# Weights of each output tile at a start of their own, 12 to 120 bytes behind a multiple of 512

## The chip, the cores and the metric

One core of one Trainium2 chip. The metric is the device time of one execution in microseconds, as the median of several runs; the kernel before has 1240.85 us (3 runs, 1239.77 to 1241.22). Beside the runs stands one profiled execution, from which all durations below are taken.

## The reference

Two residual layers over a sequence of 512 tokens of width 1024, float32. Layer 0 mixes tokens with a grouped complex state-space layer (S5), layer 1 with causal forgetting attention (FoX, 16 heads of 64). Each is followed by a gated FFN with a causal convolution of width 3 over tokens. Every sub-layer is normed, scaled and shifted by a conditioning vector, and gated back into the stream.

```python
for i in range(DEPTH):                      # DEPTH = 2
    shift, scale, gate = adaln_params(c, ada_w[i, 0], ada_b[i, 0])
    hn = modulate(h, norm_g[i, 0], shift, scale)
    m = s5_mixer(hn, ...) if i % 2 == 0 else fox_mixer(hn, ...)
    h = h + gate * m
    shift, scale, gate = adaln_params(c, ada_w[i, 1], ada_b[i, 1])
    hn = modulate(h, norm_g[i, 1], shift, scale)
    h = h + gate * conv_ffn(hn, ...)
return rmsnorm(h, final_g)

def conv_ffn(h, w_up, conv_w, conv_b, w_down):
    a, b = jnp.split(h @ w_up, 2, axis=-1)  # D_FF = 2816 each
    ap = jnp.pad(a, ((0, 0), (CONV_W - 1, 0), (0, 0)))
    a_conv = conv_b
    for i in range(CONV_W):
        a_conv = a_conv + ap[:, i:i + S] * conv_w[i]
    return (jax.nn.silu(a_conv) * b) @ w_down
```

## The kernel before

Activations stand transposed in SBUF: 128 channels on the partitions, 512 tokens along each partition, `KT` = 8 such blocks for a width of 1024. A product with a weight matrix makes one output tile of 128 channels after the other. A tile's weights are `nk` blocks of 128 x 128 floats, which lie behind each other in one room, 512 bytes of each partition per block.

Matmuls run in the type fp32r. To keep float32's precision every operand is held as two parts: `put_parts` lets ScalarE copy it into a "hi" tile (L277), and VectorE subtracts that from the original into a "lo" tile (L278). Each block of a product is then three matmuls into the same PSUM tile (`mms`, L294): hi weights with hi activations, hi with lo, lo with hi. In all but one place the weights are the loaded side (LDWEIGHTS, PEld in the profile) and the activations the moving side.

The products by kind:

- **Plain products** (`product`, middle loop, L294): one tile of weights after the other, 512 moving columns. Up-projections of some FFN tiles, all down-projections but the last ones, the gate and output of S5, queries, keys and output of FoX.
- **Head and tail of `product`**: the first tiles of some products run together, block by block, in halves of 256 tokens in most cases, so that they can follow a norm that is finished by halves. The last two or four tiles also run in halves, so that the next norm can start early.
- **Quarters** (`quarters`, L550): most up-projections of the FFN, in pairs of tiles, are made by a scheme with seven products of half size instead of eight; each is 4 blocks of 3 matmuls with 256 moving columns, 84 matmuls a pair. 15 pairs of the first FFN and 18 of the second.
- **Values of FoX** (`fox_values`, L1361): here the activations are loaded and the weights move, 256 or 272 columns at a time.

Weights come by DMA into rooms named `raw` (issued by SyncE), are split into `w_hi` and `w_lo`, and these rotate through `WB` = 5 rooms each (in the tail: 4 rooms of another pool; one split of the quarters has a room in the FFN's pool). A room has `ROOM` = 9 x 128 floats, one block more than the eight of a full tile, so a tile may begin a little behind the room's start:

```python
    t = pool.tile([P, ROOM if bufs == WB else n * w + P], F32R, name=name, tag=tag, bufs=bufs)
    return t[:, aside:aside + n * w].rearrange("p (n w) -> p n w", w=w)
```

(`part_of`.) `aside` counts floats. Before, it is 0 for the plain products and the heads, and `ASIDE` = 16, which is 64 bytes, for tails, quarters and the values. The rooms themselves begin at multiples of 512 bytes.

The order of instructions on each engine is set by the tile framework's scheduler from the order in the code, with a few explicit `issue_after` edges. The rooms and who reads and writes them set the waits between the engines.

Of the kernel before, what the change touches and what calls it, by code (L numbers as in the profile page):

```python
# [9 lines left out]
F32R = mybir.dt.float32r  # L10
# [7 lines left out]
P = 128  # L18
# [19 lines left out]
RAW, WB = 3, 5  # L38
# [22 lines left out]
    pool.tile([P, n // 4], F32, name="fill", bufs=1)  # L61


ROOM, ASIDE = 9 * P, 16


def part_of(pool, shape, name, tag, bufs, aside=0):

    _, n, w = shape
    t = pool.tile([P, ROOM if bufs == WB else n * w + P], F32R, name=name, tag=tag, bufs=bufs)  # L70
    return t[:, aside:aside + n * w].rearrange("p (n w) -> p n w", w=w)


class Trunk:
# [223 lines left out]
    def product(self, w, ms, nk, x, evac, head=0, tail=0, after=None, ticks=0, halves=HALVES, tail_pool=(), first=None, step=None):  # L298


        ms = list(ms)
        full = slice(0, S)
        if head:
            wk = first or {m: self.weights(w[m], nk) for m in ms[:head]}
            ps = {m: self.mm.tile([P, S], F32, name="mmp") for m in ms[:head]}
            for c in halves:
                for k in range(nk):
                    for m in ms[:head]:
                        self.mms(ps[m][:, c], wk[m], x, k, nk, c)
                    self.finish_norm((k + 1) * head)  # L310
                    if step:
                        step(3)
            for m in ms[:head]:
                evac(m, ps[m], full)
                self.tick(ticks)
        for m in ms[head:len(ms) - tail]:
            wk = self.weights(w[m], nk)
            ps = self.mm.tile([P, S], F32, name="mmp")
            for k in range(nk):
                self.mms(ps, wk, x, k, nk, full)  # L320
                if step:
                    step()
            evac(m, ps, full)
            self.tick(ticks)
        if tail:
            last = ms[len(ms) - tail:]
            wk = {m: self.weights(w[m], nk, *tail_pool, aside=ASIDE) for m in last}
            for c in HALVES:
                for m in last:
                    if c is HALVES[1] and m == last[tail // 2]:  # L330
                        rb = self.rms_rows(y)
                    ps = self.mm.tile([P, S // 2], F32, name="mmp")
                    for k in range(nk):
                        self.mms(ps, wk[m], x, k, nk, c)
                    evac(m, ps, c)
                if c is HALVES[0]:
                    y = after[0](c)
                else:
                    y2 = after[0](c)
                    after[1](HALVES[0], y, rb)  # L340
            self.pending = lambda: after[1](HALVES[1], y2)
# [168 lines left out]
    def quarters(self, pool, l, f, x, finish):  # L510

        nc = self.nc
        H, N = KT // 2, S // 2
        t1, t2 = HALVES
        a, b = (self.raw([P, KT, P], self.io["w_up"][l][2 * f + j]) for j in range(2))
        a11, a12, a21, a22 = a[:, :H], a[:, H:], b[:, :H], b[:, H:]
        c, d = (pool.tile([P, 2, H, P], F32, name="sums", bufs=2) for _ in range(2))
        sub = lambda o, u, v, op=ALU.subtract: nc.vector.tensor_tensor(o, u, v, op)  # L518
        w = {}
        copied = self.copied  # L520

        def parts(src, names, *where):
            hi, lo = (
                pool.tile([P, H * P + P], F32R, name=n, tag="e" + n)[:, ASIDE:ASIDE + H * P].rearrange("p (n w) -> p n w", w=P)
                if where else part_of(self.wpool, [P, len(names) * H, P], n, n, WB, ASIDE)
                for n in ("w_hi", "w_lo")
            )
            with self.behind(*copied):
                self.put_parts(hi, lo, src)
            for j, n in enumerate(names):  # L530
                w[n] = hi[:, j * H:(j + 1) * H], lo[:, j * H:(j + 1) * H]

        parts(a, ("a11", "a12"))
        sub(c[:, 0], a21, a22, ALU.add)
        sub(c[:, 1], c[:, 0], a11)
        parts(c.rearrange("p n k m -> p (n k) m"), ("s1", "s2"))
        sub(d[:, 1], a11, a21)
        sub(d[:, 0], a12, c[:, 1])
        parts(d.rearrange("p n k m -> p (n k) m"), ("s4", "s3"))
        parts(a22, ("a22",), pool)  # L540
        quarter = lambda k, t: tuple(v[:, k * H:(k + 1) * H, t] for v in x)
        xs = {"b11": quarter(0, t1), "b21": quarter(1, t1), "b22": quarter(1, t2)}
        for n, v in self.tx.items():
            xs[f"t{n}"] = v

        def times(o, wn, xn, first=True):
            (whi, wlo), (xhi, xlo) = w[wn], xs[xn]
            for k in range(H):
                for n, (wt, xt) in enumerate(((whi, xhi), (whi, xlo), (wlo, xhi))):
                    self.last_mm = nc.tensor.matmul(  # L550
                        o, wt[:, k], xt[:, k], start=(first and k == 0 and n == 0), stop=(k == H - 1 and n == 2),
                        skip_group_check=True,
                    )

        def copy(o, last=False):
            t = self.tmp.tile([P, N], F32, name="nm_h", bufs=4)
            a = nc.scalar.activation(t, o, AF.Copy)  # L557
            if last:
                self.copied = [a.ins]
            return t  # L560

        p1, p5 = (self.mm.tile([P, S], F32, name="mmp")[:, :N] for _ in range(2))
        p2, p4 = (self.aux.tile([P, S], F32, name="aux")[:, :N] for _ in range(2))
        oa, ob = (self.tmp.tile([P, S], F32, name="nm_t") for _ in range(2))
        times(p1, "a11", "b11")
        c1 = copy(p1)
        times(p5, "s1", "t1")
        c5 = copy(p5)
        times(p2, "a12", "b21")
        sub(oa[:, t1], p2, c1, ALU.add)  # L570
        times(p1, "s2", "t2", False)
        c2 = copy(p1, True)
        times(p5, "s4", "b22", False)
        sub(oa[:, t2], p5, c2, ALU.add)
        finish(2 * f, oa, slice(0, S))
        times(p4, "a22", "t4")
        c4 = copy(p4)
        times(p1, "s3", "t3", False)
        sub(ob[:, t2], p1, c5, ALU.add)
        sub(ob[:, t1], p1, c4)  # L580
        finish(2 * f + 1, ob, slice(0, S))
# [98 lines left out]
class Ew:  # L680
# [29 lines left out]
    def sub(self, a, b, out=None):  # L710
        return self.tt(a, b, ALU.subtract, out)
# [577 lines left out]
class Kernel(S5):  # L1289
# [32 lines left out]
    def fox_values(self, pool, x):  # L1322
# [10 lines left out]
        def load(qs):  # L1333

            out = {q: [] for q in qs}
            for c in range(3):
                for q in qs:
                    src = self.io["fox_v"][q - 1] if q else self.io["fox_vf"]
                    n, step = (W, 4) if q else (W + NH, 3)
                    a = c * step  # L1340
                    j = min(step, KT - a)
                    if j <= 0:
                        continue
                    with self.behind(*(self.squared if 0 in qs and c else ())):
                        hi, lo = self.split(src[:, a:a + j, :], [P, j, n], aside=ASIDE)
                    out[q] += [(hi[:, i, :], lo[:, i, :]) for i in range(j)]
            return out

        def values(qs, blocks, w, aux=()):
# [15 lines left out]
            for q, b in todo:  # L1365
# [5 lines left out]
                if q == 0:  # L1371
                    nc.vector.tensor_tensor(ft[:, b, :], ps[q, b][:, W:W + NH], bf, ALU.add)

        w = load(range(2))
        self.tick(1)
        values((0, 1), (0, 1), w)
        values((0, 1), (2, 3), w, ((0, 2), (0, 3)))
        lf = self.log_forget(ft, pool)
        for q in range(2, NV):
            values((q,), range(NB), load([q]))  # L1380
# [260 lines left out]
```

## Time and profile before

| | |
|---|---|
| median of the runs | 1240.85 us |
| profiled execution, its own time | 1233.09 us |
| its span, first to last instruction | 1231.3 us |
| busy LDWEIGHTS (PEld) | 1031.2 us |
| busy ScalarE | 606.3 us |
| DMA moved | 183.83 MB, mean 149 GB/s |
| mean granted TensorE clock | 0.995 |

Costliest single groups of the page that belong to the products:

```profile
L294 PE MATMUL mmp<-ghi,w_hi 128*128 128x512 f32 (+1 forms) x392 | 145.1, 370 | 0.0
L550 PE MATMUL mmp<-w_hi 128*128 128x256 f32 x396 | 111.4, 281 | 2.6 <-ACT nm_h L557 2.6
L278 DVE TENSOR_TENSOR w_lo<-raw,w_hi 128x1024 fp32r<-128x1024 f32 (+4 forms) x173 | 183.3, 1065 | 35.4 <-ACT w_hi L277 34.8
```

A row of groups reads: line, engine, operation, output tile <- input tiles, shapes, count | busy us, mean ns of one | idle us of the engine just before them, and who ended it. The end of a matmul is modelled, and each starts before the one ahead is marked as ended; the pace of matmuls is therefore read from the distance of their starts, in the timeline. Stretches of the program by time: S5 to about 276 us, first FFN to 600, values of FoX to 690, attention to 860, second FFN to the end.

### The profile page before, as it was taken

What the parts mean: (1) busy time and instruction counts of PE and PEld (TensorE: products, weight loads), DVE (VectorE), ACT (ScalarE), POOL (GpSimd) and SP (SyncE); (2) the same over time, 40 slices, a digit from 0 to 9 for tenths busy, and PEclk for the clock granted to TensorE, in tenths of its full rate; (3) what the DMA queues carried; (4) which work ended last, traced back from release to release, by engine and by line L of the source; (5) the groups of instructions that cost most, each with busy time, mean ns of one, the idle gap of its engine ahead of it and who ended that gap; (6) DMA issues with size and microseconds to landing.
All of it is one profiled execution on the core that took longest, in us unless ns stands there. A gap on an engine that the chain in (4) does not pass through costs nothing.

```text
span 1231.3 us, 20566 instructions
## 1 busy us (share of the span) xinstructions
PE 1200.5 (97%) x7921; PEld 1031.2 (84%) x7921; DVE 1009.0 (82%) x1872; ACT 606.3 (49%) x1137; POOL 82.7 (7%) x143
## 2 busy tenths in 40 slices
PE   7999999999999999999999999999999999999997
PEld 2466678898989899889899887878989999999987
DVE  7988886779899988799687578876899887888865
ACT  3543465335544543445443565664366554545443
POOL 0000000100000000000000243430000000000000
PEclk9999999999999999999999999999999999999999
DMA  9776668530354544444445543432122332323231
GB/s 356 244 237 215 223 225 286 192 129 35 129 178 158 192 161 160 152 168 132 125 139 190 176 150 124 147 118 94 70 69 95 120 122 77 116 86 123 95 96 69
DMA packets 74385, 183.83 MB, mean 149 GB/s; under 512 B 23231, under 2 KB 25631, under 8 KB 73263
## 3 DMA queue, kind: packets, MB, share of 16 engines
q1 hardware_dynamic: 68239, 161.02, 38.4%
q0 software_dynamic: 5760, 20.97, 5.0%
q8 instruction: 62, 1.02, 0.3%
q10 hardware_dynamic: 288, 0.52, 0.1%
q14 instruction: 36, 0.29, 0.1%
HBM read 175.57 MB, written 6.92 MB: 148 GB/s over the span
## 4 chain that ended last, share of the span: by engine, by line
PE 75%; DVE 15%; DMA 4%; issue 3%; ACT 2%; POOL 0%; SPq 0%; DVEq 0%; ACTq 0%; POOLq 0%
PE mmp L294 32%; PE mmp L550 16%; PE aux L550 6%; DVE w_lo L278 5%; PE mmp L1169 4%; PE mmp L1361 2%; DMA rawd<-in_w_down 2%; PE aux L971 2%; PE mmp L1198 2%; PE aux L1060 1%; PE aux L1500 1%; PE mmp L205 1%; PE aux L1052 1%; DVE ada_raw L247 1%; PE mmp L1109 1%
## 5 line engine op out<-in xcount | busy, mean ns | idle before, releaser
L278 DVE TENSOR_TENSOR w_lo<-raw,w_hi 128x1024 fp32r<-128x1024 f32 (+4 forms) x173 | 183.3, 1065 | 35.4 <-ACT w_hi L277 34.8
L277 ACT ACTIVATE w_hi<-raw 128x1024 fp32r<-128x1024 f32 (+4 forms) x173 | 154.8, 905 | 101.5 <-PE mmp L294 53.1
L294 PE MATMUL mmp<-ghi,w_hi 128*128 128x512 f32 (+1 forms) x392 | 145.1, 370 | 0.0
L294 PE MATMUL mmp<-glo,w_hi 128*128 128x512 f32 (+1 forms) x392 | 144.8, 369 | 0.0
L294 PE MATMUL mmp<-ghi,w_lo 128*128 128x512 f32 (+1 forms) x392 | 144.5, 369 | 0.0
L294 PE MATMUL mmp<-a_hi,w_hi 128*128 128x512 f32 (+1 forms) x376 | 138.8, 372 | 1.5 <-ACT a_hi L433 1.5
L294 PE MATMUL mmp<-a_hi,w_lo 128*128 128x512 f32 (+1 forms) x376 | 136.6, 364 | 0.3 <-DVE w_lo L278 0.3
L294 PE MATMUL mmp<-a_lo,w_hi 128*128 128x512 f32 (+1 forms) x376 | 136.2, 363 | 0.0
L550 PE MATMUL mmp<-w_hi 128*128 128x256 f32 x396 | 111.4, 281 | 2.6 <-ACT nm_h L557 2.6
L550 PE MATMUL mmp<-w_hi,w_lo 128*128 128x256 f32 x396 | 111.1, 281 | 0.7 <-DVE w_lo L278 0.7
L550 PE MATMUL mmp<-w_lo,w_hi 128*128 128x256 f32 x396 | 111.1, 281 | 0.0
L557 ACT ACTIVATE nm_h<-mmp 128x256 f32<-128x256 f32 x99 | 37.9, 384 | 131.5 <-PE mmp L550 131.5
L278 DVE TENSOR_TENSOR w_lo<-sums,w_hi 128x1024 fp32r<-128x1024 f32 x74 | 90.1, 1219 | 0.3 <-ACT w_hi L277 0.2
L294 PEld LDWEIGHTS mmp<-ghi,w_lo 128*128 128x128 f32 x392 | 74.2, 189 | 12.7 <-DVE w_lo L278 0.4
L294 PEld LDWEIGHTS mmp<-glo,w_hi 128*128 128x128 f32 x392 | 74.5, 190 | 11.1
L277 ACT ACTIVATE w_hi<-sums 128x1024 fp32r<-128x1024 f32 x74 | 76.7, 1054 | 14.4 <-DVE sums L518 11.2
L294 PEld LDWEIGHTS mmp<-ghi,w_hi 128*128 128x128 f32 x392 | 74.2, 189 | 11.4
L294 PEld LDWEIGHTS mmp<-a_hi,w_hi 128*128 128x128 f32 x376 | 70.6, 189 | 13.8 <-issue 2.6
L294 PEld LDWEIGHTS mmp<-a_hi,w_lo 128*128 128x128 f32 x376 | 70.9, 189 | 12.3 <-DVE w_lo L278 1.3
L362 DVE SCALAR_TENSOR_TENSOR h<-mmp,par,h 128x512 f32<-128x512 f32 (+1 forms) x100 | 68.1, 683 | 15.3 <-PE mmp L294 15.0
L294 PEld LDWEIGHTS mmp<-a_lo,w_hi 128*128 128x128 f32 x376 | 71.1, 189 | 9.7
L550 PEld LDWEIGHTS mmp<-w_hi 128*128 128x128 f32 x396 | 74.3, 188 | 3.0 <-ACT nm_h L557 3.0
(317 smaller groups left out, 3092.6 us busy)
## 6 DMA issues: line engine op xcount, KB each, us to landing
raw<-in_w_up SPq DMA_DIRECT2D x88, 512.0 KB, 3.3
raw<-in_ada_w SPq DMA_DIRECT2D x40, 512.0 KB, 6.3
ada_raw<-in_ada_t POOLq DMA_DIRECT2D x40, 512.0 KB, 3.9
nf<-nfd SPq DMA_DIRECT2D x8, 1152.0 KB, 6.5
raw<-in_fox_qk SPq DMA_DIRECT2D x16, 512.0 KB, 3.6
raw<-in_w_down SPq DMA_DIRECT2D x24, 320.0 KB, 3.0
rawd<-in_w_down SPq DMA_DIRECT2D x24, 256.0 KB, 3.4
raw<-in_w_down SPq DMA_DIRECT2D x16, 384.0 KB, 3.3
```

What stands on the lines that cost most here:

```text
L205: self.last_mm = nc.tensor.matmul(ps[32 * qq:32 * qq + 32, :], self.sc32[:, k, :], w[:, q * S:(q + 1) * S], start=(step is steps[0]), stop ...
L247: nc.vector.tensor_tensor_reduce(w, w, self.c_row, 1.0, 0.0, ALU.mult, ALU.add, sums[:, j:j + 1])
L277: nc.scalar.activation(hi, src, AF.Copy)
L278: return nc.vector.tensor_tensor(lo, src, hi.bitcast(F32), ALU.subtract)
L294: self.last_mm = self.nc.tensor.matmul(o, wt, xt[:, cols], start=(k == 0 and n == 0), stop=(k == nk - 1 and n == 2),)
L362: add = self.nc.vector.scalar_tensor_tensor(self.h[:, m, cols], ps, self.par[i][:, 16 + m:17 + m], self.h[:, m, cols], op0=ALU.mult, op1=A ...
L550: self.last_mm = nc.tensor.matmul(o, wt[:, k], xt[:, k], start=(first and k == 0 and n == 0), stop=(k == H - 1 and n == 2), skip_group_che ...
L557: a = nc.scalar.activation(t, o, AF.Copy)
L971: nc.tensor.matmul(ps[g2][:, j, cols], x[rows, a + j, r].rearrange("p c j -> p (c j)"), self.rr[rows, planes, q, :], start=(j == 0 and r = ...
L1169: nc.tensor.matmul(ps, w[m][:, k, :], x[:, k], start=(k == 0), stop=(k == KT - 1))
L1198: nc.tensor.matmul(gps[m], wt, xt[:, k], start=(k == 0 and part == 0 and xt is yhi), stop=(k == KT - 1 and part == 1))
L1361: self.last_mm = nc.tensor.matmul(ps[q, b][:, :n], xt[:, k, tb], wt, start=(k == 0 and i == 0), stop=(k == KT - 1 and i == 2),)
```

## The change

`ASIDE` becomes a table of eight numbers of floats: 12, 24, 40, 56, 72, 88, 104 and 120 bytes. Every tile of weights takes its entry by the number of its output tile: plain products by `m % 8` (before: 0), tails by `m % 8`, quarters by the pair's number `f % 8`, values by twice the number of the quarter of the output (before: 64 bytes for these three). Heads, and the first tiles of the S5 gate, stay at 0. All blocks of one tile share its offset.

```diff
-ROOM, ASIDE = 9 * P, 16
+ROOM = 9 * P
+ASIDE = (3, 6, 10, 14, 18, 22, 26, 30)
...
         for m in ms[head:len(ms) - tail]:
-            wk = self.weights(w[m], nk)
+            wk = self.weights(w[m], nk, aside=ASIDE[m % 8])
...
-            wk = {m: self.weights(w[m], nk, *tail_pool, aside=ASIDE) for m in last}
+            wk = {m: self.weights(w[m], nk, *tail_pool, aside=ASIDE[m % 8]) for m in last}
...
-                pool.tile([P, H * P + P], F32R, name=n, tag="e" + n)[:, ASIDE:ASIDE + H * P].rearrange("p (n w) -> p n w", w=P)
-                if where else part_of(self.wpool, [P, len(names) * H, P], n, n, WB, ASIDE)
+                pool.tile([P, H * P + P], F32R, name=n, tag="e" + n)[:, ASIDE[f % 8]:ASIDE[f % 8] + H * P].rearrange("p (n w) -> p n w", w=P)
+                if where else part_of(self.wpool, [P, len(names) * H, P], n, n, WB, ASIDE[f % 8])
...
-                        hi, lo = self.split(src[:, a:a + j, :], [P, j, n], aside=ASIDE)
+                        hi, lo = self.split(src[:, a:a + j, :], [P, j, n], aside=ASIDE[2 * q])
```

The rooms keep their sizes and addresses, and every engine has the same instructions in the same order as before; the starts of the weights inside their rooms are all that differs. (In the changed kernel the code behind the first lines stands one line later.)

## The prediction

> **What bounds the kernel now.** I read the page first, then the table of stretches, then the chain of waits, then single starts in the timeline.
>
> ```profile
> span 1231.3 us, 20566 instructions
> PE 1200.5 (97%) x7921; PEld 1031.2 (84%) x7921; DVE 1009.0 (82%) x1872; ACT 606.3 (49%) x1137; POOL 82.7 (7%) x143
> PEclk9999999999999999999999999999999999999999
> PE 75%; DVE 15%; DMA 4%; issue 3%; ACT 2%; POOL 0%; SPq 0%; DVEq 0%; ACTq 0%; POOLq 0%
> ```
>
> TensorE is busy 97% of the span at the full granted clock (the row of nines), and three quarters of the chain that ended last is matmuls. VectorE comes next with 15%. The stretches tell where each of the two sets the pace: first gated FFN, FoX values, FoX attention, and most of the second FFN.
>
> ```profile
> 276.00:600.00 324.00, 319.16 (x2039) 289.06 (x2039) 291.62 (x448) 157.50 (x249) 16.45 (x31) 1.00 0.43 147
> 600.00:690.00 90.00, 87.90 (x649) 82.72 (x648) 64.95 (x172) 36.27 (x66) 3.69 (x5) 0.98 0.47 163
> 690.00:860.00 170.00, 165.25 (x923) 135.93 (x922) 128.95 (x285) 100.93 (x235) 56.23 (x78) 1.00 0.37 127
> 920.00:1185.00 265.00, 265.00 (x1895) 249.78 (x1894) 222.17 (x333) 140.03 (x223) 0.00 (x0) 1.00 0.32 106
> ```
>
> The columns after the length are the busy times of PE, PEld, DVE, ACT and POOL. From 920 to 1185 us PE is busy in every microsecond, so there a nanosecond per matmul is a nanosecond of time. From 276 to 600 us VectorE is busy 291.62 of 324 us (90%), so part of a gain of PE would be taken back by waits on VectorE. In the chain, the second FFN is nothing but two kinds of matmul groups in turn:
>
> ```profile
> 1059.42 6.83 PE mmp L294 x30
> 1066.25 2.83 PE mmp L550 x24
> ```
>
> Columns: start, length, group, count. A plain product (L294, 512 moving columns) takes 6.83 / 30 = 228 ns per matmul, a quarter product (L550, 256 columns) 2.83 / 24 = 118 ns. Starts give these paces more exactly than the "mean ns" of a group (370 or 281), whose modelled ends overlap the next matmul.
>
> **The pace of a matmul by where its weights lie.** The change alters nothing but this. In the order that the program issues, every engine has the same rows as before, so no wait, queue, DMA or buffer moves. What moves is the byte at which a tile of weights begins in its room: before, 0 for plain products and 64 for quarters, tails and values, both behind a multiple of 512; after, 12, 24, 40, 56, 72, 88, 104 or 120. The trace has four cases of fp32r matmuls, each shown by a first and a last start. First, 512 columns, weights at 0 (15 rows, 14 steps):
>
> ```profile
> 299.72 0.39 PE L294 MATMUL mmp<-a_hi,w_lo 128*128 128x512 f32 x1
> ...
> 302.90 0.39 PE L294 MATMUL mmp<-a_lo,w_hi 128*128 128x512 f32 x1
> ```
>
> (302.90 - 299.72) / 14 = 227.1 ns. Second, 256 columns, weights at 0 (head of the second FFN, 25 steps):
>
> ```profile
> 876.57 0.28 PE L294 MATMUL mmp<-a_hi,w_hi 128*128 128x256 f32 x1
> ...
> 879.56 0.28 PE L294 MATMUL mmp<-a_lo,w_hi 128*128 128x256 f32 x1
> ```
>
> 2.99 / 25 = 119.6 ns. Third, 256 columns, weights at 64 (quarters, 26 steps):
>
> ```profile
> 1141.53 0.28 PE L550 MATMUL mmp<-a_hi,w_hi 128*128 128x256 f32 x1
> ...
> 1144.59 0.28 PE L550 MATMUL aux<-a_hi,w_lo 128*128 128x256 f32 x1
> ```
>
> 3.06 / 26 = 117.7 ns. Fourth, the values of FoX, where the weights are the moving side, at 64, and the activations the loaded side, at 0 (23 steps):
>
> ```profile
> 655.79 0.28 PE L1361 MATMUL mmp<-w_hi,a_lo 128*128 128x256 f32 x1
> ...
> 658.40 0.28 PE L1361 MATMUL mmp<-w_hi,a_lo 128*128 128x256 f32 x1
> ```
>
> 2.61 / 23 = 113.5 ns. From the first two, 256 more columns cost 227.1 - 119.6 = 107.5 ns, so a column costs 0.42 ns, and at place 0 a matmul has about 12.1 ns on top of its columns at either width. At 64 it has 117.7 - 107.5 = 10.2 ns, and in the fourth case 6.0 ns. The reader is to see that the piece on top is not fixed: it takes three values in one trace, at one clock and one width, and the place of the operands is what differs. The weight loads run beside the stream:
>
> ```profile
> 1141.53 0.19 PEld L550 LDWEIGHTS mmp<-a_lo,w_hi 128*128 128x128 f32 x1
> 1141.65 0.19 PEld L550 LDWEIGHTS mmp<-a_hi,w_lo 128*128 128x128 f32 x1
> ```
>
> The load of the next weights starts together with each matmul (1141.53 both), so both read SBUF in the same 110 ns, and a matmul of 256 columns leaves a load hardly any slack. That two such reads hinder each other by their addresses is my reading, not something these rows prove.
>
> **The Trainium skill at this place.** "SBUF — State Buffer", section "Who interferes with whom", gives TensorE two read ports, independent of each other, and "TensorE: Matmul & The Clock Gate", section "Back-to-back issue gap", gives 512 columns as 512 / 2.4 + 2.5, an estimate of 215.8 ns. By the two, places would not matter at all; the trace has 227.1 ns and three values on top of the columns, so it does not bear the gap out and leaves the ports in doubt.
>
> **The terms.** Counts follow from the loops and the stretches hold them.
> - Plain products, middle loop, 0 to the eight places: FFN tiles that are neither head, tail nor quarters 732 + 588, gate of S5 72, its output 144, q and k of FoX 384, its output 48: 1968 matmuls of 512 columns, 447 us of PE. No row shows 512 columns at another place than 0. Bounds: all that lies on top of the columns goes, 12.1 x 1968 = -23.8 us; or, on the other side, one matmul gains what a 256-wide one can lose between its best and worst case, 119.6 - 113.5 = 6.1 ns, +12.0 us. The nearest row is the step from 0 to 64 at 256 columns, 119.6 to 117.7 = 1.9 ns: -3.7 us. I take that.
> - Quarters (33 x 84 = 2772) and tails (432), 64 to the eight places: 3204 matmuls of 256 columns. Bounds: down to 113.5, -4.2 x 3204 = -13.5 us; up to 119.6, +1.9 x 3204 = +6.1 us. The middle is where they are; I take 0.
> - Values of FoX: 384 with the moving side moved; between 0 and 119.6 - 113.5 = 6.1 ns each, +2.3 us at most. Taken as 0.
> - The writes of weights by ScalarE (L277) and VectorE (L278), and VectorE's reads, now begin at such places too.
>
> ```profile
> L278 DVE TENSOR_TENSOR w_lo<-raw,w_hi 128x512 fp32r<-128x512 f32 x33 | 22.6, 686 | 0.0
> L278 DVE TENSOR_TENSOR w_lo<-rawd,w_hi 128x512 fp32r<-128x512 f32 x24 | 16.5, 686 | 3.0 <-ACT w_hi L277 2.9
> L362 DVE SCALAR_TENSOR_TENSOR h<-mmp,par,h 128x512 f32<-128x512 f32 x76 | 56.6, 747 | 13.0 <-PE mmp L294 12.9
> L602 DVE SCALAR_TENSOR_TENSOR conv<-nm_t,conv_wb,conv 128x511 f32<-128x511 f32 x33 | 24.7, 747 | 5.0 <-ACT conv L600 5.0
> L602 DVE SCALAR_TENSOR_TENSOR conv<-nm_t,conv_wb,conv 128x510 f32<-128x510 f32 x33 | 24.6, 744 | 0.2
> ```
>
> The first two rows are the same split at 64 and at 0: 686 ns both. The last two begin 4 and 8 bytes into their tile, and take 747 and 744 against 747 ns for a full one at its start. So VectorE minds neither. ScalarE is bound the same way by its slack (157.50 busy of 324 us). Cost 0; were each of some 250 splits 5 ns longer, 1 us in all, hidden by PE where PE is full.
>
> The sum on PE is -3.7 us. What becomes time: all of it in the second FFN (588 of the 1968), about 0.7 elsewhere, where VectorE is near its limit or the chain changes engines: 0.3 x 1 + 0.7 x 0.7 = 0.8, so -3.0 us. The profiled execution took 1233.1 us (span 1231.3); its forecast is 1230.1. The runs have a median 7.8 us above it (1240.85), so **1237.9 us**. What is late next is still PE; VectorE's 32 us of slack in the first FFN is more than any gain here.
>
> **Rivals.**
> 1. No dependence for wide matmuls. For it: 512 columns outlast the load twice over, so a disturbed load could be absorbed, and in the values of FoX the same code at the same places also runs at another pace for a while:
>
> ```profile
> 628.48 0.28 PE L1361 MATMUL mmp<-w_hi,a_lo 128*128 128x256 f32 x1
> 628.59 0.28 PE L1361 MATMUL mmp<-w_hi,a_hi 128*128 128x256 f32 x1
> 628.71 0.28 PE L1361 MATMUL mmp<-w_lo,a_hi 128*128 128x256 f32 x1
> 628.83 0.28 PE L1361 MATMUL mmp<-w_hi,a_lo 128*128 128x256 f32 x1
> 628.95 0.28 PE L1361 MATMUL mmp<-w_hi,a_hi 128*128 128x272 f32 x1
> ```
>
> These are 110 to 120 ns apart, at fixed places, so the pace has a history and is not the place alone. Against it: at 0 the piece on top is 12.1 ns at both widths. All terms near 0: 1240 to 1242 us.
>
> 2. Slower: the new places make loads of 256-wide matmuls longer, since none but 0 and 64 has been seen and neither 12 nor 24 is a multiple of 64. The load is what such a matmul waits for, so it is felt at once there, and from 3.0 / (3204 x 0.9) = 1.0 ns per matmul on it outweighs the gain of the forecast. With the pace of the worst case seen, 119.6 ns, it is +6.1 us, nine tenths of it felt: +5.5, and 512 columns unchanged: 1246 us. For it: no row has a place that is not a multiple of 64. Against: VectorE minds no such start.
> "SBUF — State Buffer", section "Door 1: The DMA port swizzle", in its note on cachelines, has lines of 16 bytes and a penalty for each crossing to a new one. By it 512 bytes that begin at 8 or 12 behind a line touch 33 lines, not 32: an estimate of 1/32 of a load, some 3.5 ns, 11 us for the quarters and tails. No trace here shows it, since 0 and 64 both begin a line.
>
> 3. Much faster: the eight places keep load and stream out of each other's way. At 215.0 and 113.5 ns it is -23.8 - 13.5 = -37.3 us on PE, 0.8 of it in time: 1211 us. If half of the places do so, 1226 us. For it: 113.5 ns is seen, so 6 ns on top is possible. Against: the change from 0 to 64 brought 1.9 ns only.
>
> That the change does nothing is excluded for addresses (30 floats fit into the 128 spare ones of a room, 9 x 128 against 8 x 128), and is rival 1 for times.
>
> **Chances.** Forecast (a few us faster, 1231 to 1238) 0.32; rival 1 0.27; rival 2 0.25; rival 3 wholly or by half 0.16. Faster by over 0.2% (2.5 us, about what a measurement of this kernel can tell from none) is the forecast and rival 3: 0.48; within it 0.27; slower 0.25. The likeliest's own range is 1231 to 1239. For 8 in 10 I leave out the full rival 3 and the far end of rival 2: 1217 to 1248.
>
> **What would show it.** Right: steps of plain products in the second FFN near 225 ns instead of 227, quarters still near 118, stretch 920 to 1185 shorter by 1 to 2 us, PE still full there. Rival 1: 227 at every tile. Rival 2: quarter groups of 24 longer than 2.83 us. Rival 3: groups of 24 near 2.72 us, or plain steps under 220 ns, and VectorE named more often as what PE waits for. The forecast is wrong if paces differ by place with signs that cancel otherwise than I took them, which groups by output tile would tell.

## The result and the profile after

The changed kernel is slower: 1243.73 us (median of 18 runs) against 1238.11 us for the kernel before (18 runs), ratio 1.0045, 95% interval [1.0028, 1.0061]. One of the 18 runs of the changed kernel took 1710.62 us at a granted clock of 0.648; the ratio leaves it out, and the other 17 lie between 1239.2 and 1252.21 us. The profiled execution of the changed kernel took 1240.36 us.

Head of the page of the changed kernel:

```profile
span 1238.6 us, 20566 instructions
PE 1209.9 (98%) x7921; PEld 1032.6 (83%) x7921; DVE 1008.7 (81%) x1872; ACT 606.5 (49%) x1137; POOL 82.3 (7%) x143
```

The span grew by 7.3 us, and PE's busy time by 9.4 us. The busy time of DVE, ACT, POOL and of the weight loads is the same to 1.4 us or better. So it is the matmuls themselves that take longer.

The chain of waits of the changed kernel in the second FFN (start, length, group, count; every line number is one more than before):

```profile
1002.02 8.40 PE mmp L295 x36
...
1020.44 8.28 PE mmp L295 x36
...
1032.95 2.83 PE mmp L551 x24
...
1055.50 2.74 PE mmp L551 x24
1059.61 2.72 PE mmp L551 x24
...
1118.62 1.47 PE aux L551 x12
1120.09 2.92 PE mmp L551 x24
```

Each group can be set beside its place, since the loops fix which tile follows which. The first group is two down-projection tiles at 72 and 88 bytes: 8.40 / 36 = 233.3 ns a matmul. The same two tiles before, at 0:

```profile
996.62 8.19 PE mmp L294 x36
```

8.19 / 36 = 227.5 ns. The second group has tiles at 104 and 120: 230 ns. Of the quarters (L551), those at 56 keep 2.83 us for 24, those at 88 are down to 2.72 (113.3 ns), and those at 24 are up to 2.92 (121.7 ns). So the pace depends on the place, differently at 512 columns and at 256, and the eight places are not alike.

For all matmuls I took the distance of each start to the next one from the trace and grouped it by the place of its weights. Steps longer than 250 ns at 512 columns or 140 ns at 256 are left out; they are waits. Summed over the same matmuls, before and after:

| matmuls | count | before us | after us | difference |
|---|---|---|---|---|
| L294, 512 columns | 2038 | 463.9 | 472.1 | +8.3 |
| quarters, L550 | 2757 | 323.8 | 324.8 | +1.1 |
| heads and tails, 256 columns | 677 | 79.9 | 80.4 | +0.4 |
| values, 256 columns | 283 | 32.5 | 34.0 | +1.5 |

PE pays about 11 us, of which the span shows 7.3 and the medians of the runs 5.6.

A mean can hide two paces. Pair by pair, the quarters of the kernel before, all at 64, take 117.8 ns in 29 of the 33 pairs, 113.7 and 114.0 in two, and something between in the other two. The first experiment comes back to this.

### The profile page after: what moved, and what is told of

It reads as the page before. It is cut to its first block, busy times and chain, and to the rows that moved or that the text cites. A ratio compares the mean times of both kernels' runs of the same rounds, so it can differ in the third digit from the quotient of the medians.

```text
span 1238.6 us, 20566 instructions
## 1 busy us (share of the span) xinstructions
PE 1209.9 (98%) x7921; PEld 1032.6 (83%) x7921; DVE 1008.7 (81%) x1872; ACT 606.5 (49%) x1137; POOL 82.3 (7%) x143
## 4 chain that ended last, share of the span: by engine, by line
PE 68%; issue 14%; DVE 10%; DMA 5%; ACT 1%; POOL 1%; SPq 0%; DVEq 0%; POOLq 0%; ACTq 0%
PE mmp L295 26%; PE mmp L551 15%; PE aux L551 6%; PE mmp L1170 4%; PE mmp L1362 3%; DVE w_lo L279 3%; PE aux L972 2%; PE mmp L1199 2%; PE aux L1061 1%; PE aux L1501 1%; PE mmp L206 1%; PE aux L1053 1%; DMA rawd<-in_w_down 1%; DVE ada_raw L248 1%; DMA ada_raw<-in_ada_t 1%
## 5 line engine op out<-in xcount | busy, mean ns | idle before, releaser
L551 PE MATMUL mmp<-w_hi 128*128 128x256 f32 x396 | 111.2, 281 | 2.4 <-ACT nm_h L558 2.4
L551 PE MATMUL mmp<-w_hi,w_lo 128*128 128x256 f32 x396 | 111.0, 281 | 0.7 <-DVE w_lo L279 0.7
L551 PE MATMUL mmp<-w_lo,w_hi 128*128 128x256 f32 x396 | 111.0, 280 | 0.0
L551 PEld LDWEIGHTS mmp<-w_hi 128*128 128x128 f32 x396 | 74.5, 188 | 2.9 <-ACT nm_h L558 2.9
```

Of the source, the lines that this page charges most:

```text
L551: self.last_mm = nc.tensor.matmul(o, wt[:, k], xt[:, k], start=(first and k == 0 and n == 0), stop=(k == H - 1 and n == 2), skip_group_che ...
```

## The experiments

All start from the kernel before, with a place of its own for each kind of tile. The names in the edits: `PLAIN`, `TAILS`, `QUARTERS` and `VALUES` are tables in floats, read by `m % 8`, `m % 8`, `f % 8` and `q`. Three theories stood against each other at first: that the place of the loaded weights decides (place theory), that it costs when neighbouring tiles differ (spread theory), and that a load pays for each 16-byte line that it touches (theory of lines, from the rival on the record).

**Plain products alone.**

```diff
+PLAIN, TAILS, QUARTERS, VALUES = (3, 6, 10, 14, 18, 22, 26, 30), (16,) * 8, (16,) * 8, (16,) * 4
...
-            wk = self.weights(w[m], nk)
+            wk = self.weights(w[m], nk, aside=PLAIN[m % 8])
```

> Only the plain products (512 columns) get the eight places; quarters, tails and values stay at 64. Place theory (the pace of a matmul depends on where its loaded weights begin, with another map for each width): the eight 512-column paces of the changed kernel come back (227 at 12 and 120 up to 233 at 56 to 104 ns), +8 us on PE, two thirds of it in time: +5.4 us, ratio 1.0044. Spread theory (neighbouring tiles at different places disturb each other's reads and writes, whatever the place): the loss is shared by all kinds of tiles, so less than half of it here, ratio about 1.002.

Measured: 1241.3 against 1235.89 us, ratio 1.0035 [1.0014, 1.0056]. The steps at 512 columns sum to +8.25 us, as in the changed kernel. The plain products carry most of the loss.

The quarters, which were not moved, got 3.1 us shorter in this trace (mean step 116.3 ns, 117.4 before). The reason is visible pair by pair: 11 pairs run at 113.4 to 114.2 ns and 20 at 117.8 or 117.9. Here is the chain of this run for two pairs of the second FFN, two lines each, and below it the first line of the first of these pairs in the kernel before:

```profile
959.89 2.72 PE mmp L551 x24
963.97 2.72 PE mmp L551 x24
...
977.75 2.83 PE mmp L551 x24
981.99 2.83 PE mmp L551 x24
```

```profile
954.65 2.83 PE mmp L550 x24
```

The same pair, at the same place, thus takes 2.83 us for 24 in one kernel and 2.72 in the other. At 64 bytes the place leaves two paces open. What picks one of them is not shown; of the program, only the places of the plain products differ between the two. A sum over quarters at 64 can therefore differ by some 3 us between kernels that treat them alike.

**All the others alone.**

```diff
+PLAIN, TAILS, QUARTERS, VALUES = (0,) * 8, (3, 6, 10, ..., 30), (3, 6, 10, ..., 30), (3, 10, 18, 26)
```

> Only quarters, tails and values get the eight places; plain products stay at 0. Place theory: +1.5 us at the 256-column products and +1.4 us at the values on PE, so +1 to +3 us, ratio 1.0015. Spread theory: more than half of the loss, ratio 1.0025 or more. My record's rival of longer loads for quarters: the whole loss, 1.0045.

Measured: ratio 1.0011 [0.9986, 1.0036]; steps at 512 columns +0.3 us, quarters +0.8, heads and tails +0.5, values +1.5. A loss of about this size was expected, but the interval takes in none at all. That longer loads in the quarters are the cause is excluded: the whole loss would be 1.0045.

**Multiples of 16 bytes.**

```diff
+PLAIN, TAILS, QUARTERS, VALUES = (0, 4, 8, 12, 16, 20, 24, 28), (0, 4, 8, ..., 28), (0, 4, 8, ..., 28), (0, 8, 16, 24)
```

> All kinds of tiles get the multiples of 16 bytes from 0 to 112 in turn (values 0, 32, 64, 96), read by place from the trace. Theory of lines (a load that does not begin on a 16-byte line costs more): all eight 512-column paces are 227 ns as at 0. Place theory: the map has no regard for lines; places 64 to 96 are on the plateau of 233 ns like 56 to 104, and at 256 columns 80 or 96 come near the 113.5 ns of 88.

In the chain of this kernel, tiles at 16 and 32, and later at 64 and 80:

```profile
972.11 8.39 PE mmp L295 x36
...
1004.69 8.37 PE mmp L295 x36
```

233.1 and 232.5 ns, though each of these begins on a 16-byte line. The theory of lines falls. At 16 bytes, too, there are two paces: of the 12 tiles there, five take 226.6 or 226.7 ns, the others 232.8 to 233.3. The place theory missed as well in one point: at 256 columns 80 and 96 bytes have 118.7 and 117.4 ns, not near the 113.5 of 88.

**Quarters and tails at 88.**

```diff
+PLAIN, TAILS, QUARTERS, VALUES = (0,) * 8, (22,) * 8, (22,) * 8, (16,) * 4
```

> Quarters and tails all at 88 bytes, plain products at 0 and values at 64 as before. Place theory: 256-column steps of 113.5 to 114 ns instead of 117.4, 3204 x 3.5 = -11 us on PE, ratio 0.992 (0.989 to 0.995). Spread theory: no spread, no difference, 1.000. Theory of lines: 88 is no multiple of 16, so 1.000 or more.

Measured: 1231.82 against 1235.89 us, ratio 0.9964 [0.9937, 0.9991]. Quarters have a mean step of 113.8 ns (117.4 before), and PE saves 10.0 us there and 1.0 at the tails. The mechanism is as expected, the gain in time is less than half of it. Of the 33 pairs, 31 run at 113.3 to 114.1 ns and two at 116.7, so 88 holds the shorter pace that 64 has now and then. The groups of the page of this kernel by form, mean ns of one next to the busy time (a modelled end lies some 163 ns after the next start, so differences of these means are differences of pace):

```profile
L551 PE MATMUL mmp<-w_hi,w_lo 128*128 128x256 f32 x396 | 109.5, 277 | 0.9 <-DVE w_lo L279 0.9
L551 PE MATMUL mmp<-a_hi,w_lo 128*128 128x256 f32 x264 | 73.2, 277 | 0.9 <-DVE w_lo L279 0.9
L551 PE MATMUL mmp<-a_lo,w_hi 128*128 128x256 f32 x264 | 73.0, 277 | 0.0
```

277 ns here, 281 before, whether a form (`w_hi`) or the activations (`a_hi`, `a_lo`) move.

**The activations moved by 64 bytes.** The same kernel, with fills that shift `a_hi` and `a_lo` and leave all weights where they are:

```diff
         fill(self.small, 1440 - 1024)
+        fill(self.act, 64)
+        fill(self.wpool, 448)
```

> The normed activations a_hi and a_lo begin 64 bytes behind a multiple of 512; quarters and tails have their weights at 88, plain products at 0, as in the run before with quarters at 88. Theory of two reads (the distance between the moving operand's and the loaded operand's place decides): products with a_hi or a_lo moving now have distances of 24 and of -64: 256 columns go from 113.8 to 118 to 120 ns, 512 columns from 227 to some 230 to 234 ns; products with ghi, glo or the forms moving, still at 0, keep 227 and 113.8 ns. Theory of the load alone (only the loaded operand's place decides): 227 and 113.8 ns for both kinds.

The same groups of this kernel (two lines further down in the code):

```profile
L553 PE MATMUL mmp<-w_hi,w_lo 128*128 128x256 f32 x396 | 109.5, 277 | 0.7 <-DVE w_lo L281 0.7
L553 PE MATMUL mmp<-a_hi,w_lo 128*128 128x256 f32 x264 | 75.1, 284 | 0.8 <-DVE w_lo L281 0.8
L553 PE MATMUL mmp<-a_lo,w_hi 128*128 128x256 f32 x264 | 75.2, 285 | 0.0
```

Quarters with a form moving keep 277 ns; those with the shifted activations moving take 284 and 285. In the chain of this kernel, twelve with activations moving:

```profile
1007.80 1.47 PE aux L553 x12
```

122.5 ns. The weights lie at 88 in both. Their distance to the activations is 24 now, and the mean step is 121.0 ns where the changed kernel had 120.7 for weights at 24 and activations at 0. At 512 columns, weights at 0: 229.3 ns with shifted activations moving, 227.6 and 228.2 with `ghi` and `glo`, which were not shifted. The values of FoX, where the shifted side is loaded and the weights at 64 move, have a distance of 0 now and go to 119.6 ns (114.9 in the kernel before, 116.4 in the run with quarters at 88), the pace of equal places elsewhere. So the place of the weights alone does not decide: with weights that stay, the pace changes with the place of the activations, and the distance between the two operands accounts for all these cases. The evidence is one shift, of 64 bytes, in a single run (1233.0 us).

**Beyond 128 bytes.**

```diff
+PLAIN, TAILS, QUARTERS, VALUES = (32, 48, 64, 80, 96, 112, 128, 30), (16,) * 8, (32, 48, 64, 80, 96, 112, 128, 30), (16,) * 4
```

> Plain products and quarters at 128, 192, 256, 320, 384, 448, 512 and 120 bytes in turn; tails and values at 64. Read by place. If the map repeats every 128 bytes: 512 columns take 227 ns at 128, 256, 384 and 512 and 231 to 236 ns at 192, 320 and 448, as at 0 and 64; 256 columns about 120 at the former, 116 to 118 at the latter. If it repeats only every 512 bytes: 227 at 512 alone of the multiples, and the others are open. If place is only 'on a multiple of 512 or not': all but 512 are at 231 to 236 ns.

Mean steps at 512 and at 256 columns, in ns: 128 bytes 232.7 and 119.7; 192: 229.4 and 117.8; 256: 228.3 and 119.8; 320: 233.3 and 117.8; 384: 232.4 and 119.4; 448: 230.3 and 117.1; 512: 228.0 and 119.8. So neither 128 nor 512 is the period: 256 is like 0, 320 like 64 (233.1, 116.3), 384 like 128, 448 like 192. The shift of the activations fits too: a distance of -64 is 192 by this period, and 229.3 and 229.4 ns agree at 512 columns, as do 117.7 (the heads of that run) and 117.8 at 256. The period is read from means at multiples of 64; at other distances it was not tried.

**In steps of four bytes.**

```diff
+PLAIN, TAILS, QUARTERS, VALUES = (1, 2, 3, 4, 5, 29, 30, 31), (19, ..., 26), (19, 20, 21, 22, 23, 24, 25, 26), (16,) * 4
```

> Plain products at 4, 8, 12, 16, 20, 116, 120 and 124 bytes, quarters and tails at 76 to 104 bytes in steps of 4, values at 64. Read by place. If the pace is a smooth function of the distance between two read positions: 512 columns rise from 227 ns at 4 to 231 at 20 without jumps, and are 227 from 116 to 124; 256 columns have a dip some 12 bytes wide around 88, with 84 and 92 under 116 ns. If single bytes decide (a matter of which words share a line): 88 alone is near 113.5 and its neighbours 118 or more.

The chain of this kernel, quarters at 76, 84 and 88:

```profile
985.42 2.73 PE mmp L551 x24
989.51 2.72 PE mmp L551 x24
...
1017.44 2.88 PE mmp L551 x24
...
1035.79 2.75 PE mmp L551 x24
1039.89 2.72 PE mmp L551 x24
```

The pace jumps from word to word: 113.6 at 76, 118.7 at 80, 119.9 at 84, 113.7 at 88, 118.3 at 92 and 119.9 at 100. At 512 columns it is 232.3 at 4, 230.9 at 8, 230.9 at 12 (a mixture of 224 and 236), 233.2 at 16 (230.6 in the run with multiples of 16), 230.6 at 116, 227.8 at 120, 232.3 at 124. The expectation of a smooth function fails, and 76 was foreseen by neither expectation.

**The other half of the 256 bytes.**

```diff
+PLAIN, TAILS, QUARTERS, VALUES = (34, 42, 45, 38, 54, 58, 61, 50), (16,) * 8, (34, 42, 45, 38, 54, 58, 61, 50), (16,) * 4
```

> Plain products and quarters at 136, 168, 180, 152, 216, 232, 244 and 200 bytes in turn; tails and values at 64. Read by place, in the half of the 256 bytes that was not looked at. Theory of two reads with a period of 256 bytes says only that the paces stay between 224 and 236 ns at 512 columns and 113 and 121 ns at 256. If the map were mirrored about 0, then 168 and 180 (the mirrors of 88 and 76) are the good ones at 256 columns, near 113.7, and 136 (of 120) at 512, 227; if not, these are like their neighbours.

At 256 columns all eight lie between 117.0 and 119.9 ns (168: 117.9, 180: 117.0), at 512 columns between 229.4 and 233.2 (136: 233.2). At 512 columns the map is not mirrored: 136 is nothing like 120. At 256 columns this stays open, since the 117.9 at 168 is the mean of one pair at 113.7 and two at 120.0, so the mirror of 88 has its pace too, but does not hold it. No mean of these eight places is better than that of 0 for plain products or of 88 and 76 for quarters.

**Plain products all at 88.**

```diff
+PLAIN, TAILS, QUARTERS, VALUES = (22,) * 8, (16,) * 8, (16,) * 8, (16,) * 4
```

> Plain products all at 88, the rest at 64 as before: the cost of the change's plain products taken at its worst place for each tile. Theory of two reads: 512 columns go from 227.6 to 233.3 ns, 1968 x 5.7 = +11.2 us on PE, against +8.3 in the changed kernel; 1.4 times the loss of the run with only the plain products changed, ratio about 1.005 (1.003 to 1.008). Spread theory: no spread, 1.000.

The chain of this kernel beside the one before (8.19 and 2.83):

```profile
1006.30 8.40 PE mmp L295 x36
1014.70 2.83 PE mmp L551 x24
```

Measured: 1244.36 against 1238.05 us, ratio 1.0046 [1.0023, 1.0069]. One and the same place for all costs about as much as eight different ones, so the spread theory falls. On PE it is +10.8 us, near the +11.2 expected. That it is 1.4 times the loss of the run with the plain products alone can't be told from intervals this wide.

**The heads at 88 too**, the version that the others point to: plain products at 0, all 256-column products with loaded weights at 88.

```diff
+PLAIN, TAILS, QUARTERS, VALUES = (0,) * 8, (22,) * 8, (22,) * 8, (16,) * 4
...
-            wk = first or {m: self.weights(w[m], nk) for m in ms[:head]}
+            wk = first or {m: self.weights(w[m], nk, aside=22 * (len(halves) - 1)) for m in ms[:head]}
```

> As the run with quarters and tails at 88, and the heads that run in halves of 256 columns at 88 too, plain products at 0. Place theory: another 288 matmuls from 119.8 to about 114 ns, -1.6 us on PE; ratio to the kernel before 0.995 (0.993 to 0.998), the first FFN's share of the gain being taken back by waits on VectorE and DMA as in that run. If the gain of that run was chance: 1.000.

Measured: 1229.11 against 1237.77 us, ratio 0.994 [0.9916, 0.9965]: faster than the kernel before and the changed one. Heads and tails together go to a mean of 114.1 ns. The chain of its second FFN:

```profile
1006.82 2.72 PE mmp L551 x24
1012.26 8.18 PE mmp L295 x36
```

Paces by place, mean ns of a step (activations at a multiple of 512 in all of these):

| bytes | 0 | 12 | 16 | 24 | 32 | 40 | 48 | 56 | 64 | 72 | 80 | 88 | 96 | 104 | 112 | 120 |
|---|---|---|---|---|---|---|---|---|---|---|---|---|---|---|---|---|
| 512 columns | 227.6 | 229.7 | 230.6 | 230.9 | 232.9 | 233.0 | 233.1 | 233.1 | 233.1 | 233.4 | 231.8 | 233.3 | 234.0 | 233.1 | 232.9 | 227.3 |
| quarters | 119.8 | 116.8 | 118.3 | 120.7 | 118.3 | 119.1 | 117.9 | 117.8 | 116.3 | 118.4 | 118.7 | 114.1 | 117.4 | 118.5 | 119.9 | 119.4 |

(0 at 512 columns from the kernel before; 12, 24, 40, 56, 72, 88, 104 and 120 from the changed one; the rest from the run with multiples of 16. Where the table has 12 and 16 at 512 columns, and 24, 64 and 104 at 256, the mean covers tiles or pairs at two or more paces.)

## Why the prediction was wrong

**The step that failed** is the first term: "The nearest row is the step from 0 to 64 at 256 columns, 119.6 to 117.7 = 1.9 ns: -3.7 us. I take that." It carries a gain from 256 columns over to 512. There, 0 is among the best places, and leaving it costs 5 to 6 ns at five of the eight places (40 to 104), 2 to 3 at 12 and 24, and nothing at 120. The term measured +8.3 us (4.05 ns x 2038, a count that takes in about 110 matmuls that were not moved). The upper bound put beside it, +12.0 us, held.

The sign that the prediction named for being right was a stretch from 920 to 1185 us shorter by 1 to 2 us; the same matmuls took 2.0 us longer there.

**What bounds the kernel** was right, and so was that only the paces of matmuls would move: DVE's and ACT's busy times agree before and after to 0.3 us.

**Quarters and tails at 0 us** were nearly right in sum (+1.1 and +0.4 us), and hid a mixture: 88 gains 3.3 ns on 64, 24 loses as much. The sum is luck in part, since the unmoved quarters of the first experiment differ by 3.1 us. The reading behind these terms was too simple: the 117.7 ns at 64 and the 113.5 of the values are not the paces of two arrangements, for the quarters at 64 show both. **The values at 0** were 1.5 us too low, inside the bound of 2.3 us.

**The factor 0.8** from PE to time was on the high side: 7.3 of 11.2 us in the profiled pair, half in the medians. By stage, from the starts of the same matmuls in both traces: the first FFN grows by 3.1 us for 3.8 on PE, the stretch from 860 to 1185 us by 2.7 for 2.7, but FoX (600 to 860) by 0.1 us for some 3 us. The chain of the kernel before is cut up most there: 362 pieces in 260 us, against 300 in the 324 us of the first FFN and 164 in the 325 us from 860 on. That the longer steps vanish in waits that were there fits this, but no run tried it.

**The rivals.** Number 1, no dependence at 512 columns, is refuted by every run that moved plain products; its argument that the pace has a history is borne out by the quarters at 64. Number 2 gave 1246 us, a ratio of 1.0042 to the median shown then, which is about what was measured; but its mechanism is not the cause, so the number is luck. It laid the loss on the quarters with plain products unchanged, and it is the reverse. The Trainium skill's note in "SBUF — State Buffer", section "Door 1: The DMA port swizzle", that each crossing to a new 16-byte line pays a penalty, does not set these paces: multiples of 16 are in the mean as slow as the rest at 512 columns, and 120 and 88, which are no multiples, are among the best. Number 3, load and stream out of each other's way, is real at 256 columns for 76 and 88, where the step comes down to 113.6 to 114.1 ns, about the 113.5 that it named; 64 and 168 have this pace in some pairs only. At 512 columns its 215 ns was not found at any place tried.

**Why a distance matters.** The rows of the prediction showed that a load starts together with the matmul ahead of it. The run with shifted activations shows that the pace changes with the distance of the two operands while the weights stay. That the stream and the load hinder each other when both read SBUF is the reading that fits; no run shows the reads themselves. The Trainium skill ("SBUF — State Buffer", section "Who interferes with whom") has the two read ports of TensorE as independent; the runs do not bear that out for the pace, which changes by 7 ns in a step of 114 (113.8 ns at a distance of 88, 121.0 at 24). How the distance is turned into lost time, why places 256 bytes apart are alike, why 64 has two paces, and why 88 is good at 256 columns and bad at 512, stays open: no run here separates the widths from the starts of the loads.

**Why the gain of 88 is not whole.** In the version with heads, PE saves some 4 us in the first FFN, and the stretch gets no shorter: it ends 1.6 us later against its start. Steps over 15 ns above their pace, from 280 to 600 us, sum to about 12 us, 6.5 before. Waits of the weight loads in that stretch, of this version and then of the kernel before (who waited, for whom: us, times, longest):

```profile
PEld mmp L551 <- ACT nm_h L558: 3.6, 3, 2.9
PEld mmp L295 <- DVE w_lo L279: 2.8, 4, 1.1
PEld mmp L551 <- DVE w_lo L279: 2.7, 4, 1.1
```

```profile
PEld mmp L550 <- ACT nm_h L557: 3.3, 3, 2.6
PEld mmp L550 <- DVE w_lo L278: 1.4, 2, 0.9
PEld mmp L294 <- DVE w_lo L278: 1.4, 4, 0.7
```

The lo parts from VectorE come late for longer, 5.5 us against 2.8, in eight waits against six. That fits VectorE's 90% there, but it makes up only a part of the difference, and that it is the cause was not tried. From 860 to 1185 us PE saves 7.5 us, and 7.2 of it is in the time.

## What to carry to other kernels

Where matmuls follow each other without a gap, the byte at which an operand begins was worth up to 6 ns a matmul here, and the distance to the other operand is what to vary: measure it by the distance of starts, for each width of its own, and carry no figure from one width to another. A table with a place for each tile is a good probe, since one profile then shows all places side by side, but read it tile by tile, for a place can have two paces; as a setting it pays the mean of good and bad ones. Before the gain is counted, look at which stretches have PE in every microsecond: only there does a nanosecond of pace stay a nanosecond.

## What was not expected of the hardware

- The pace of fp32r matmuls with weights loaded for each one depends on the distance of moving and loaded operand: 227 to 234 ns (means) at 512 columns, 113.6 to 121 ns at 256, at the full granted clock.
- At 256 columns single words decide: 113.6 at 76 bytes, 118.7 at 80, 119.9 at 84, 113.7 at 88.
- Distances that differ by 256 bytes have the same mean pace within 2 ns, in four pairs at two widths; by 128 bytes they differ (512 columns: 227.6 at 0, 232.7 at 128).
- One place can have two paces, each held over a whole tile or pair: quarters at 64 run at 113.4 or 117.8 ns (two pairs of 33 near the shorter in the kernel before, 11 in a run that moved only plain products), a tile of 512 columns at 16 at 226.6 or 233.3. The values of FoX at 64 had a mean of 114.9 ns in the kernel before and 115.3 to 117.7 in seven runs that changed nothing of them.
